# A hybrid streaming encoder layer: a small table moved behind four large slots, and three subtractions moved from VectorE to GpSimd

## The chip, the cores and the metric

One core of one Trainium2 chip runs the whole layer. The metric is the device time of one execution in microseconds; lower is better.

## The reference

One layer of a trunk with three gated branches, for 1024 prompt rows and 32 sample rows of width 1024, in float32:

```python
xn = rmsnorm(h, norm_mix)
proj = xn @ w_in
u_a, u_b, v_b, q, k, v, gates = jnp.split(proj, IN_SPLITS, axis=-1)
y_a, st_re, st_im = s5_mixer(u_a, ...)
y_b, vn_b = sgu_mixer(u_b, v_b, sgu_norm, sgu_w, sgu_b)
...
y_c = o.transpose(0, 2, 1, 3).reshape(bsz, L, SB_WIDTH).astype(h.dtype)
g = jax.nn.sigmoid(gates.astype(jnp.float32)).reshape(bsz, L, N_BRANCH, D_MODEL)
merged = (g[:, :, 0] * (y_a @ w_branch_a) + g[:, :, 1] * (y_b @ w_branch_b)
          + g[:, :, 2] * (y_c @ w_branch_c))
h = h + (merged.astype(h.dtype) @ w_out).astype(h.dtype)
gu = rmsnorm(h, norm_ffn) @ w_gate_up
h = h + ((jax.nn.silu(gate) * up) @ w_down).astype(h.dtype)
```

`o` is stick-breaking attention of 8 heads of 64 over 1024 positions: the weight of position s for query t is `exp(log_sigmoid(z_s) + sum of log_sigmoid(-z) over the positions between s and t)`, and it multiplies the values.

## The kernel before

**Split operands.** Every dense product is made of three matmuls (`mm3`, lines 143 to 146): an operand a is stored as a high part, rounded to float32r, and a low part a - high; the product is ah·bh + ah·bl + al·bh. A split costs one copy on ScalarE for the high part and one subtraction for the low part, on VectorE (DVE) or GpSimd (POOL).

**Stages.** In this order: normalise and turn x; project values, queries and keys, the S5 branch and the gated MLP branch; attention, with the remaining dense work (keys, queries, gates ahead) dealt out between its steps by `fill`; the gates and branch outputs (`gates`, per half of the rows); the output projection (`out_proj`); the up projection (`up_tile`, 22 tiles, each of seven products for two chunks of 256 and 272 columns); the down projection (`down_groups`, 11 groups of 256 hidden columns, the last two done together) and the final norm. A scheduler sets the order on each engine from priorities; TensorE's order of the up projection is written out by hand.

**Attention.** For each pair of heads hp, each quarter tp of the queries and each head h2 of the pair there is a unit: scores (lines 824 to 828), sigmoid into `om` on ScalarE (line 830), a running product backwards over `om` on VectorE (the scan of line 832), turning of `om` on TensorE (line 854) into PSUM, high parts `wth` or `wd` on ScalarE (line 862), low parts `wtl` or `wd` on VectorE (line 863), products with the values (lines 871 and 872). The sum over the weights is rewritten by parts, so what multiplies the weights is not the values but differences of neighbouring values. `differences` (lines 785 to 791) makes them once for each of the 8 heads: line 787 subtracts shifted values (128x512), line 789 does the four diagonal blocks with their last row, line 790 rounds the high part on ScalarE, line 791 makes the low part (128x768) into `vt`. The raw values `va` have one buffer, `vt` three. After the second head of each pair, 16 times in all, lines 884 to 887 add the two halves of the output (64x512), split it, and store it with two DMAs on SP's queue (line 890); `yo` has one buffer.

```python
for i in range(2):
    ahead(i)
...
for i, u in enumerate(units):
    ahead(i + 2)
```

`ahead` loads the queries of the unit two places on and, when it is the first of its head, its keys and values; the differences of that head are recorded at the next call.

**Memory of the later stages.** Behind each other in each partition lie the pool `late` (`hS`, `mt2`, `gb`, `ss2`, `htmp`) and the pool `hy` of four slots of 17408 bytes. `ss2` holds 20 numbers in each partition: the sums of squares of the rows for the norm in front of the up projection. It takes 80 bytes, rounded up to 96. In the built program the four slots `hy` begin at bytes 140512, 157920, 175328 and 192736, each 32 past a multiple of 64; the four slots of the older pool `hx` begin at 17536, 34944, 52352 and 69760, multiples of 128; the rings of split weights `wh` and `wl` begin at multiples of 128 too. In `hy` lie `y` and `m` of the gates (`m` is the stationary operand of the output projection), `xo2` to `xo5` of the up projection (moving operands; `xo0`, `xo1` and `xo6` lie in `hx`), and `act` of ten of the eleven groups of the down projection, the stationary operand there. The first group's `act` is put into `hx` (`load_act(0, wa, hx)`). The stationary `xn` of the values' projection lies in `hx`.

Of the kernel before, what the change touches and what calls it, by code (L numbers as in the profile page):

```python
# [9 lines left out]
F32 = mybir.dt.float32  # L10
# [38 lines left out]
def trunk_kernel(ctx: ExitStack, tc: tile.TileContext,  # L49
# [7 lines left out]
    v, g, s, pe, sp = nc.vector, nc.gpsimd, nc.scalar, nc.tensor, nc.sync  # L57
    PSUM, DRAM = bass.MemoryType.PSUM, bass.MemoryType.DRAM

    def pool(name, bufs=1, space=None):  # L60
        if space is DRAM:
            return tc.tile_pool(name=name, bufs=bufs, space=space)
        if space is not None:
            return tc.tile_pool(name=name, bufs=bufs, space=space, reuse_waits="tile")
        return tc.tile_pool(name=name, bufs=bufs, reuse_waits="tile")
# [138 lines left out]
    with ExitStack() as ph1:  # L204
# [6 lines left out]
        def ps_tile(tag):  # L211
            return ps1.tile([128, 512], F32, name="p_" + tag, tag=tag)
# [550 lines left out]
        def attention(at, qk_tasks):  # L763
# [20 lines left out]

            def differences(va, vt):
                vb = vt[:, :, 1, :].bitcast(F32)
                v.tensor_sub(va[:, 0:8], va[:, 0:8], vb[:, 0:8])

                v.scalar_tensor_tensor(va[:, 8:12], vb[:, 8:12], last, va[:, 8:12], op0=OP.mult, op1=OP.add)
                s.activation(vt[:, :, 0, :], va, AF.Copy)  # L790
                v.tensor_sub(vt[:, :, 1, :], va, vt[:, :, 0, :].bitcast(F32))

            heads = {}

# [43 lines left out]
            def stage_b(hp, tp, h2, ws):  # L838
                vt = heads[hp, h2][1]
                if h2 == 0:  # L840
                    avs[hp, tp] = ps_tile("av")
                av2 = avs[hp, tp]
                av = av2[:, 256 * h2:256 * h2 + 256]
                hl = {}

                def turn(p):

                    pt = ps_tile("t")
                    diag = p == tp
                    for e in range(4):  # L850
                        if diag and e == 0:
                            continue
                        sb, tt = 2 * p + 1 - e // 2, e % 2
                        pe.transpose(pt[:, 128 * e:128 * e + 128], ws[tt][:, 128 * sb:128 * sb + 128], ident)
                    lo = 128 if diag else 0
                    if diag:
                        wh, wl = diags[cnt[0] % 2]
                        cnt[0] += 1
                    else:
                        wh = at.tile([128, 512], F32R, name="wth", bufs=2)  # L860
                        wl = at.tile([128, 512], F32R, name="wtl", bufs=2)
                    s.activation(wh[:, lo:512], pt[:, lo:512], AF.Copy)
                    v.tensor_sub(wl[:, lo:512], pt[:, lo:512], wh[:, lo:512].bitcast(F32))
                    hl[p] = wh, wl

                def apply(p):
                    wh, wl = hl.pop(p)
                    for i in range(2):
                        b = 8 + p if p == tp and i == 0 else 2 * p + 1 - i
                        lhs = vt[:, b].rearrange("p l d -> p (l d)")  # L870
                        pe.matmul(av, lhs, wh[:, 256 * i:256 * i + 256], start=(p == 0 and i == 0), stop=False)
                        pe.matmul(av, lhs, wl[:, 256 * i:256 * i + 256], start=False, stop=(p == tp and i == 1))

                for p in range(tp + 1):
                    turn(p)
                    yield 0.44
                    if p:
                        apply(p - 1)
                        yield 0.44
                apply(tp)  # L880
                if h2:
                    yo = at.tile([64, 2, 512], F32R, name="yo")
                    ty = yo[:, 1].bitcast(F32)
                    s.activation(ty, av2[64:128], AF.Copy)
                    v.tensor_add(ty, av2[0:64], ty)
                    s.activation(yo[:, 0], ty, AF.Copy)
                    v.tensor_sub(yo[:, 1], ty, yo[:, 0].bitcast(F32))
                    o = 256 * (tp % 2)
                    for e in range(2):
                        sp.dma_start(y_d[4 + hp][tp // 2].rearrange("l p t -> p l t")[64 * e:64 * e + 64, :, o:o + 256],  # L890
                                     yo[:, :, 256 * e:256 * e + 256].bitcast(F32))
                yield 0.44
# [9 lines left out]
            def ahead(i):  # L902

                if i < len(units):
                    hp, tp, h2 = units[i]
                    new = (hp, h2) not in heads
                    if new:
                        finish(qk_tasks[hp])
                        heads[hp, h2] = [load_head(hp, h2)]
                    load_q(hp, tp, h2)  # L910
                    if new:
                        while raw_values:
                            differences(*raw_values.pop())
                        pair = load_values(hp, h2)
                        heads[hp, h2].append(pair[1])
                        raw_values.append(pair)
                        return
                while raw_values:
                    differences(*raw_values.pop())
# [5 lines left out]
            for i, u in enumerate(units):  # L925
                ahead(i + 2)
                nxt, done = None, True
                if i + 1 < len(units):
                    nxt = stage_a(*units[i + 1])
                    done = False  # L930
                for c in stage_b(*u, ws):
                    fill(ratio * c)
                    if not done:
                        try:
                            wn, c = next(nxt)
                            fill(ratio * c)
                        except StopIteration:
                            done = True
                if not done:
                    for wn, c in nxt:  # L940
                        fill(ratio * c)
                if nxt is not None:
                    ws = wn
                if i == 30:
                    sample_attention(at)
# [124 lines left out]
    late = ctx.enter_context(pool("late", 1))  # L1070
# [8 lines left out]

    H = [None, None]  # L1080

    ss2 = late.tile([128, 20], F32, name="ss2")
    v.memset(ss2, 0.5)

    def h_rows(b):
# [441 lines left out]
```

## Time and profile before

| | |
|---|---|
| time, median of 3 runs | 1766.96 us (1764.95 to 1767.31) |
| the profiled execution's own time | 1750.41 us |
| its span | 1748.7 us |
| TensorE matmul busy (PE) | 1642.2 us, 94% |
| VectorE busy (DVE) | 974.5 us, 56% |
| ScalarE busy (ACT) | 603.3 us, 35% |
| GpSimd busy (POOL) | 626.5 us, 36% |

The page gives the busy time of each engine and cuts the span into 40 slices of 43.7 us. A share of busy time is a mean over stages with different limits. Matmuls are pipelined: the record of one lasts longer than the distance from its start to the next one's start, so the pace is read from starts. PE is TensorE's matmul, PEld its loading of the stationary operand.

### The profile page before, as it was taken

Reading aid. Unit: us, or ns where it says so; the run is one execution under the profiler, and the core shown is the slowest. Engines: PE = TensorE matmul, PEld = TensorE weight load, DVE = VectorE, ACT = ScalarE, POOL = GpSimd, SP = SyncE. Lnnn points to the kernel's source line nnn. Section 1 sums busy time; section 2 is a strip of 40 time slices with the busy share of each in tenths; the row PEclk is TensorE's granted clock in tenths of the full one; section 3 lists DMA queues with packets and bytes.
Section 4 is the critical chain, followed back from the end, with each engine's and each line's share of the span. In section 5 each row is a group of like instructions: output and inputs, shape, how many; then the busy total and the mean of one; then the engine's idle time right before and its main releaser. Section 6 shows DMA issues by size and latency. Waiting matters only on the chain. (4 is left out here: it accounts for less than half of the span.)

```text
span 1748.7 us, 28070 instructions
## 1 busy us (share of the span) xinstructions
PE 1642.2 (94%) x10949; PEld 1489.0 (85%) x10949; DVE 974.5 (56%) x1864; ACT 603.3 (35%) x1111; POOL 626.5 (36%) x378
## 2 busy tenths in 40 slices
PE   6989998999889899999999798999999999899997
PEld 6978896778677798899999798999999998677775
DVE  7963513512899730910284756666555556566545
ACT  4322332233667532223225543333333323222114
POOL 2310211433102223434456754333333326544434
PEclk9999999999999999999999899999999999999999
DMA  7454245356656427854361223322222226322212
GB/s 225 108 134 93 84 137 129 97 169 192 172 150 160 119 80 239 261 193 133 92 214 49 81 79 109 94 77 74 74 80 85 83 85 233 109 75 79 67 37 88
DMA packets 271421, 211.57 MB, mean 121 GB/s; under 512 B 68340, under 2 KB 244504, under 8 KB 270776
## 3 DMA queue, kind: packets, MB, share of 16 engines
q1 hardware_dynamic: 242728, 194.56, 37.9%
q10 hardware_dynamic: 28560, 15.21, 2.9%
q8 instruction: 86, 1.41, 0.4%
q14 instruction: 47, 0.39, 0.1%
HBM read 153.83 MB, written 55.30 MB: 120 GB/s over the span
## 5 line engine op out<-in xcount | busy, mean ns | idle before, releaser
L118 POOL TENSOR_TENSOR wl<-raw,wh 128x1024 fp32r<-128x1024 f32 x120 | 303.3, 2535 | 735.1 <-ACT wh L117 695.0
L117 ACT ACTIVATE wh<-raw 128x1024 fp32r<-128x1024 f32 x120 | 126.3, 1058 | 331.1 <-PE p L146 146.4
L144 PE MATMUL p<-xo,wl 128*128 128x256 f32 (+1 forms) x616 | 178.0, 289 | 5.9 <-DVE fs L1353 3.2
L144 PE MATMUL p<-xo,wh 128*128 128x256 f32 (+1 forms) x616 | 177.5, 288 | 4.0 <-ACT wh L1308 2.3
L146 PE MATMUL p<-xo,wl 128*128 128x256 f32 (+1 forms) x616 | 178.0, 289 | 3.3 <-POOL wl L1309 3.3
L146 PE MATMUL p<-xo,wh 128*128 128x256 f32 (+1 forms) x616 | 178.0, 289 | 2.2 <-POOL wh L1309 2.2
L145 PE MATMUL p<-xo,wh 128*128 128x256 f32 (+1 forms) x616 | 176.6, 287 | 1.2 <-POOL xo L1247 1.2
L145 PE MATMUL p<-xo,wl 128*128 128x256 f32 (+1 forms) x616 | 176.5, 287 | 0.0
L144 PE MATMUL p_d<-xnh,wh 128*128 128x272 f32 (+1 forms) x464 | 157.8, 340 | 6.5 <-ACT wh L117 3.5
L146 PE MATMUL p_d<-xnh,wl 128*128 128x272 f32 (+1 forms) x464 | 155.4, 335 | 5.0 <-POOL wl L118 5.0
L145 PE MATMUL p_d<-xnl,wh 128*128 128x272 f32 (+1 forms) x464 | 155.2, 334 | 0.0
L144 PE MATMUL p<-wh,act 128*128 128x512 f32 x352 | 140.7, 400 | 5.9 <-DVE htmp L136 3.6
L1481 DVE TENSOR_TENSOR hd<-p,hd 128x512 f32<-128x512 f32 x160 | 107.1, 684 | 70.1 <-PE p L146 69.7
L145 PE MATMUL p<-wl,act 128*128 128x512 f32 x352 | 140.7, 400 | 2.4 <-POOL wl L118 2.4
L146 PE MATMUL p<-wh,act 128*128 128x512 f32 x352 | 140.5, 399 | 0.0
L1309 POOL TENSOR_TENSOR wh<-raw,wh 128x512 fp32r<-128x512 f32 x59 | 79.3, 1347 | 139.0 <-ACT wh L1308 137.6
L1309 POOL TENSOR_TENSOR wl<-raw,wl 128x512 fp32r<-128x512 f32 x58 | 78.6, 1358 | 135.2 <-ACT wl L1308 134.6
L144 PEld LDWEIGHTS p<-xo,wl 128*128 128x128 f32 x616 | 117.7, 191 | 7.0 <-DVE fs L1353 3.4
L144 PEld LDWEIGHTS p<-xo,wh 128*128 128x128 f32 x616 | 117.9, 191 | 4.8 <-ACT wh L1308 2.6
L146 PEld LDWEIGHTS p<-xo,wl 128*128 128x128 f32 x616 | 117.8, 191 | 3.7 <-POOL wl L1309 3.7
L146 PEld LDWEIGHTS p<-xo,wh 128*128 128x128 f32 x616 | 117.8, 191 | 2.5 <-POOL wh L1309 2.4
L145 PEld LDWEIGHTS p<-xo,wh 128*128 128x128 f32 x616 | 118.3, 192 | 1.4 <-POOL xo L1247 1.4
(463 smaller groups left out, 4415.2 us busy)
## 6 DMA issues: line engine op xcount, KB each, us to landing
raw<-in_w_in_dram SPq DMA_DIRECT2D x66, 512.0 KB, 4.0
raw<-in_w_gate_up_dram SPq DMA_DIRECT2D x46, 512.0 KB, 4.4
ra<-act_d SPq DMA_DIRECT2D x22, 528.0 KB, 4.1
raw<-in_w_down_dram SPq DMA_DIRECT2D x22, 512.0 KB, 3.8
q<-q_d SPq DMA_DIRECT2D x64, 128.0 KB, 2.9
raw<-in_w_out_dram SPq DMA_DIRECT2D x16, 512.0 KB, 6.0
act_d<-fs SPq DMA_DIRECT2D x44, 128.0 KB
act_d<-fa SPq DMA_DIRECT2D x44, 128.0 KB, 3.9
```

The lines of the kernel that those rows point to most:

```text
L117: s.activation(wh, raw, AF.Copy)
L118: g.tensor_sub(wl, raw, wh.bitcast(F32))
L144: pe.matmul(ps, ah, bh, start=start, stop=False)
L145: pe.matmul(ps, ah, bl, start=False, stop=False)
L146: pe.matmul(ps, al, bh, start=False, stop=stop)
L1309: eng.tensor_sub(lo, src, hi.bitcast(F32))
L1481: v.tensor_add(hr[:, cs], ps, hr[:, cs])
```

## The change

Three subtractions of the attention go to GpSimd (`g`) in place of VectorE (`v`): the differences of shifted values (line 787), their low parts (line 791) and the low parts of the attention outputs (line 887). Their number and shapes stay: 8, 8 and 16. The table `ss2` gets a pool of its own, opened after `hy`, so that it lies behind the four slots.

```diff
             def differences(va, vt):
                 vb = vt[:, :, 1, :].bitcast(F32)
-                v.tensor_sub(va[:, 0:8], va[:, 0:8], vb[:, 0:8])
+                g.tensor_sub(va[:, 0:8], va[:, 0:8], vb[:, 0:8])
...
-                v.tensor_sub(vt[:, :, 1, :], va, vt[:, :, 0, :].bitcast(F32))
+                g.tensor_sub(vt[:, :, 1, :], va, vt[:, :, 0, :].bitcast(F32))
...
-                    v.tensor_sub(yo[:, 1], ty, yo[:, 0].bitcast(F32))
+                    g.tensor_sub(yo[:, 1], ty, yo[:, 0].bitcast(F32))
...
-    ss2 = late.tile([128, 20], F32, name="ss2")
+    ss2 = ctx.enter_context(pool("late2", 1)).tile([128, 20], F32, name="ss2")
```

In the built program `ss2` then lies at byte 210048, in memory that the last of the four buffers of `om` held before (it was memory of `k32`), and `hy` begins 96 bytes earlier: 140416, 157824, 175232 and 192640, all multiples of 128. `hx`, the rings and the tiles of the attention stay where they were. TensorE's order changes in the attention alone, where dense matmuls fall between other steps than before.

On VectorE, at the start of the attention (`om` is the running product of line 832, `wd` and `wtl` low parts of turned weights, `va` and `vt` raw values and their differences):

```order
 L832 SCALAR_TENSOR_TENSOR om<-om 128x256
 L863 TENSOR_TENSOR wd_3835<-p_t,wd_3834 128x384
-L787 TENSOR_TENSOR va<-va,vt 128x512
 L789 SCALAR_TENSOR_TENSOR va<-vt,last,va 128x256
-L791 TENSOR_TENSOR vt<-va,vt 128x12x64
 L832 SCALAR_TENSOR_TENSOR om<-om 128x128
 L832 SCALAR_TENSOR_TENSOR om<-om 128x256
 L863 TENSOR_TENSOR wd_3837<-p_t,wd_3836 128x384
-L787 TENSOR_TENSOR va<-va,vt 128x512
 L789 SCALAR_TENSOR_TENSOR va<-vt,last,va 128x256
-L791 TENSOR_TENSOR vt<-va,vt 128x12x64
```

Line 789 stays on VectorE and stands between scans, now without the subtraction in front of it and the one behind it.

On GpSimd, from the start of the attention (`wl` is the low part of a unit of dense weights, line 118):

```order
-L118 TENSOR_TENSOR wl<-raw,wh 128x1024 x9
+L118 TENSOR_TENSOR wl<-raw,wh 128x1024
+L787 TENSOR_TENSOR va<-va,vt 128x512
+L791 TENSOR_TENSOR vt<-va,vt 128x12x64
+L787 TENSOR_TENSOR va<-va,vt 128x512
+L791 TENSOR_TENSOR vt<-va,vt 128x12x64
+L887 TENSOR_TENSOR yo<-yo 64x512 x2
+L787 TENSOR_TENSOR va<-va,vt 128x512
+L791 TENSOR_TENSOR vt<-va,vt 128x12x64
+L887 TENSOR_TENSOR yo<-yo 64x512
+L118 TENSOR_TENSOR wl<-raw,wh 128x1024
```

GpSimd had nothing but weights' low parts here; now 787, 791 and 887 stand in its one line with them.

On SP's queue, at the third and fourth quarter of the second pair of heads (`q` are queries, `va` and `vt` values, `y_d` the stored outputs):

```order
 L781 DMA va<-v_d_73 128x8x64
-L806 DMA q_4832<-q_d_64 64x2x256
 L890 DMA y_d_0_121<-yo 64x2x256 x2
-L806 DMA q_4832<-q_d_64 64x2x256
+L806 DMA q_4832<-q_d_64 64x2x256 x2
+L806 DMA q_4917<-q_d_65 64x2x256 x2
 L782 DMA va<-v_d_73 128x4x64
-L806 DMA q_4917<-q_d_65 64x2x256 x2
 L781 DMA vt<-v_d_73 128x8x64
+L890 DMA y_d_0_121<-yo 64x2x256 x2
```

The stores of the outputs have moved by a place or two against the loads of queries and values.

## Rows read from the trace of the kernel before

**Rows 1.** Page, busy tenths of VectorE in 40 slices of the span.
```profile
DVE  7963513512899730910284756666555556566545
```

**Rows 2.** Windows: start:end, length, busy us (instructions) of PE, PEld, DVE, ACT, POOL; granted clock.
```profile
444.00:582.00 138.00, 121.29 (x815) 101.25 (x813) 132.85 (x151) 91.70 (x183) 22.07 (x5) 0.99 0.62 158
582.00:655.00 73.00, 69.08 (x522) 64.79 (x523) 34.21 (x51) 29.48 (x59) 17.51 (x22) 0.98 0.30 89
```

**Rows 3.** Waits from 444 to 582 us: us in total, times, longest.
```profile
PEld p_av L872 <- DVE wtl L863: 15.8, 20, 3.0
```

**Rows 4.** Timeline of PE, down projection: start, duration (us).
```profile
1464.46 0.39 PE L144 MATMUL p<-wh,act 128*128 128x512 f32 x1
...
1475.11 0.39 PE L146 MATMUL p<-wh,act 128*128 128x512 f32 x1
...
1550.06 0.40 PE L146 MATMUL p<-wh,act 128*128 128x512 f32 x1
...
1561.07 0.39 PE L145 MATMUL p<-wl,act 128*128 128x512 f32 x1
```

**Rows 5.** Timeline of PE, output projection and values' projection.
```profile
750.29 0.28 PE L144 MATMUL p<-wh,m 128*128 128x256 f32 x1
...
783.89 0.28 PE L144 MATMUL p<-wh,m 128*128 128x256 f32 x1
...
59.28 0.28 PE L144 MATMUL p_av<-wh,xnh 128*128 128x256 f32 x1
...
62.13 0.28 PE L144 MATMUL p_d<-wh,xnh 128*128 128x256 f32 x1
```

**Rows 6.** Timeline of PE, up projection: one product from xo4, one from xo6.
```profile
1175.44 0.29 PE L144 MATMUL p<-xo,wh 128*128 128x272 f32 x1
...
1176.93 0.28 PE L144 MATMUL p<-xo,wh 128*128 128x256 f32 x1
...
1178.38 0.29 PE L144 MATMUL p<-xo,wh 128*128 128x272 f32 x1
...
1179.88 0.28 PE L144 MATMUL p<-xo,wl 128*128 128x256 f32 x1
```

**Rows 7.** Groups of VectorE, 444 to 582 us: count, busy us, mean ns.
```profile
L887 DVE TENSOR_TENSOR yo<-yo 64x512 fp32r<-64x512 f32 x12 | 8.1, 672 | 0.9 <-ACT yo L886 0.6
...
L791 DVE TENSOR_TENSOR vt<-va,vt 128x768 fp32r<-128x768 f32 x6 | 6.7, 1121 | 0.1
L787 DVE TENSOR_TENSOR va<-va,vt 128x512 f32<-128x512 f32 x6 | 5.1, 853 | 0.0
```

**Rows 8.** Groups of GpSimd by shape, whole span: count, busy us, mean ns.
```profile
L1309 POOL TENSOR_TENSOR wh<-raw,wh 128x512 fp32r<-128x512 f32 x59 | 79.3, 1347 | 139.0 <-ACT wh L1308 137.6 <-issue 1.4
...
L1390 POOL TENSOR_TENSOR act<-ra,act 128x1024 fp32r<-128x1024 f32 x22 | 53.1, 2421 | 14.4 <-ACT act L1389 14.4
L1475 POOL TENSOR_TENSOR hS<-hS,htmp 32x512 f32<-32x512 f32 x20 | 25.6, 1278 | 12.6 <-DVE htmp L136 11.5 <-DVE rs_m L170 1.1
```

**Rows 9.** Timeline of VectorE, rows beside GpSimd's five and two undisturbed ones.
```profile
476.32 2.02 DVE L791 TENSOR_TENSOR vt<-va,vt 128x768 fp32r<-128x768 f32 x1
478.27 2.58 DVE L832 TENSOR_TENSOR_SCAN om<-om 128x128 f32<-128x128 f32 x1
...
522.36 0.41 DVE L832 TENSOR_TENSOR_SCAN om<-om 128x128 f32<-128x128 f32 x1
...
552.84 2.27 DVE L832 TENSOR_TENSOR_SCAN om<-om 128x1024 f32<-128x1024 f32 x1
...
559.19 2.63 DVE L832 TENSOR_TENSOR_SCAN om<-om 128x1024 f32<-128x1024 f32 x1
...
567.77 3.28 DVE L832 TENSOR_TENSOR_SCAN om<-om 128x1024 f32<-128x1024 f32 x1
...
572.01 1.74 DVE L787 TENSOR_TENSOR va<-va,vt 128x512 f32<-128x512 f32 x1
```

**Rows 10.** Groups of GpSimd, 444 to 582 us.
```profile
L118 POOL TENSOR_TENSOR wl<-raw,wh 128x1024 fp32r<-128x1024 f32 x5 | 22.1, 4433 | 122.9 <-ACT wh L117 122.9
```

## The prediction

> **What bounds the kernel now.** I read the page's engine slices first, then the windows of the two places that the change touches, then the waits, then single rows. TensorE is busy for nearly all of the span (the table above), so a gain has to shorten TensorE's own work or take away one of its waits. VectorE's slices [rows 1] show one stretch, the 11th to the 14th slice, in which VectorE is full: that is the attention stage. The windows give its edges [rows 2]: from 444 to 582 us VectorE is busy 132.85 of 138.00 us and GpSimd 22.07, while TensorE has 121.29; from 582 to 655 VectorE is down to 34.21 of 73.00 us. So in the first stretch VectorE sets the pace, in the second it has time to spare. TensorE's longest wait in the stretch says the same [rows 3]: 15.8 us of weight loads waiting for line 863, VectorE's low parts of the turned weights. The last stages (gates, output projection, up and down projections) are TensorE's alone, and there a gain can only come from faster matmuls.
>
> **The change, part one: the 96 bytes.** The table `ss2` leaves the pool in front of the `hy` slots, and the built program moves all four slots from 32 bytes past a multiple of 64 to multiples of 128. The `hx` slots are multiples of 128 in both. No instruction is added or moved by this. The trace of before holds a natural experiment: the same matmuls run out of both kinds of slot.
>
> Down projection, stationary operand `act`. The first group's `act` lies in `hx`: from 1464.46 to 1475.11 there are 47 steps from start to start, 10.65 / 47 = 0.2266 us each. The fourth group's lies in `hy`: 1550.06 to 1561.07, 47 steps again, 11.01 / 47 = 0.2343 us [rows 4]. Ten of the eleven groups have their `act` in `hy`, with 16 products of 6 matmuls each for the prompt's rows: 960 matmuls x 0.0077 = 7.4 us less, if address is the cause. TensorE has no gaps inside these groups, so it counts in full. The 64-column matmuls of the sample rows are few (80); I leave them at nothing, at most 80 x 0.0077 = 0.6 us.
>
> Output projection, stationary operand `m`, 256 columns, in `hy`: 288 steps from 750.29 to 783.89, 33.60 / 288 = 0.1167 us. The same shape with `xn` stationary out of `hx`: 24 steps from 59.28 to 62.13, 2.85 / 24 = 0.1188 us [rows 5]. Here the slot that is off by 32 bytes is the quicker one. There are 768 such matmuls: 768 x 0.0021 = 1.6 us more.
>
> Up projection, moving operand `xo`, 272 columns: twelve matmuls out of `xo4` (`hy`) take 1176.93 - 1175.44 = 1.49 us, twelve out of `xo6` (`hx`) 1179.88 - 1178.38 = 1.50 [rows 6]. Five of the seven products of a tile use `hy` slots for this chunk: 22 x 5 x 0.01 = 1.1 us more. The 256-column products and the gates' `y` operands have no clean pair of rows; I take them at nothing, within 1.2 us either way (576 gate matmuls at the 0.0021 of rows 5).
>
> Sum of part one: -7.4 + 1.6 + 1.1 = -4.7 us. Its ends: 0 if the address is not the cause, -8 if only the down projection reacts.
>
> **Part two: VectorE gives three subtractions to GpSimd.** In the full stretch it loses 12 of line 887 (8.1 us), 6 of 791 (6.7) and 6 of 787 (5.1), 19.9 us together [rows 7]. Two of these hold a collision each, about 1.1 us, which would hit the next instruction instead (below), so 19.9 - 2.1 = 17.8 us of pace. The other moved ones (4 of line 887, 2 of each of the others) lie outside, where VectorE has time: nothing.
>
> GpSimd gets the work at its own price. Its 32x512 subtraction takes 1278 ns and its 128x512 one 1347 [rows 8]; for 64x512 I take 1.3 us, for line 787 1.35. Line 791 has 768 elements, half way between 1347 and the 2421 ns of 1024: 1.89. In the stretch: 12 x 1.3 + 6 x 1.35 + 6 x 1.89 = 35.0 us, on an engine that is busy 22.07 of 138.
>
> That is not free for VectorE. In the stretch, five low parts of weights (line 118) ran on GpSimd [rows 10], 2.4 us each when nothing is in the way (the same size in rows 8). Five VectorE rows with both inputs in SBUF grew beside them [rows 9]: line 791 at 476.32 (2.02; the other five average 0.94 by rows 7), the scan at 478.27 (2.58, against 0.41 at 522.36), the scans at 559.19 and 567.77 (2.63 and 3.28, against 2.27 at 552.84), line 787 at 572.01 (1.74, the other five 0.68). That is 1.08 + 2.17 + 0.36 + 1.01 + 1.06 = 5.7 us for 5 x 2.4 = 12.0 us of GpSimd: 47%. In between, rows that read PSUM (lines 863, 885) ran on untouched, which is why it isn't all of it. So the 35.0 us cost VectorE 35.0 x 0.47 = 16.5, and part two is -17.8 + 16.5 = -1.3 us. Its ends: -16.7 (no collisions; TensorE's busy time leaves no more, 138.00 - 121.29) and +17.2 (35.0 - 17.8, each GpSimd instruction costs all its length). I keep to the 47%, since those rows are this stretch and this pair of engines.
>
> The Trainium skill (SBUF — State Buffer, section "Who interferes with whom") states that a VectorE instruction with two SBUF inputs and a GpSimd instruction that reads SBUF lock each other out for the whole instruction; the five rows agree in kind, and by that rule alone, with a two-input instruction always next, part two would be the +17.2 of the upper end.
>
> What else the move touches. Line 789 now waits on VectorE for GpSimd's line 787, and behind it stand scans; 787 needs only its two loads, and GpSimd reaches it early, so I take nothing. Line 791 comes later by 1.89 - 0.94 = 0.95 us; TensorE waits for no `vt` in rows 3's view, and the heads are loaded two units ahead: nothing, but up to 0.95 + 0.67 us (787's share) at each of the three places where a head pair begins, 4.9 us, if that lead is used up. The output `yo` has one buffer: line 884 on ScalarE may wait for its stores if line 887 stands behind a 791. Each of the 32 stores on SP's queue now waits for GpSimd, and query loads stand behind them; these are for two units on. Nothing for both, by the same lead. The `memset` of `ss2` now waits for the last buffer of `om` instead of `k32`; behind it on VectorE are gates that TensorE reaches only after more dense work: nothing.
>
> **Sum.** -4.7 - 1.3 = -6.0 us. Against the profiled execution, 1750.41 - 6.0 = 1744.4; that execution lies 0.9% below the median of the runs, 1766.96, so the same 6.0 us there give **1761.0 us**, 0.34% less. About 0.2%, 3.5 us, is what a measurement of this kernel can tell from no change.
>
> **The rivals.** *The address is not the cause.* Part one is then 0, and the time 1766.96 - 1.3 = 1765.7. For it: the first group could be quick because its slot lies far from the weights, and the up projection's rows hardly differ. Against it: rows 5 and 6 differ by slot too, and with opposite sign, as one cause of distance would not make them. The Trainium skill (TensorE: Matmul & The Clock Gate, section "Wait — 56ns, not 53.3ns?") gives the spacing of warm matmuls as columns / 2.4 GHz plus some 2.5 ns, with no address in it; by that rule this rival holds, but the rows at 0.2266 and 0.2343 have the same columns and both lie above it. Chance 0.20.
>
> *GpSimd's instructions cost VectorE nearly all their length*, as the scan at 478.27 did (2.17 of 2.4). It happens where a scan follows a scan and no PSUM row stands between. At all of it the time is 1766.96 - 4.7 + 17.2 = 1779.5. It ends slower by over 3.5 us from a share of (17.8 + 4.7 + 3.5) / 35.0 = 74%. Against it: four of the five rows lost 15 to 45%. Chance 0.17.
>
> *The collisions hide behind PSUM rows.* The new instructions are shorter than 2.4 us, and two PSUM rows cover 1.3. At a share of 15%, the smallest of the five, part two is -17.8 + 5.2 = -12.6 and the time 1749.7. Against it: TensorE and ScalarE would have to follow at once. Chance 0.13.
>
> **How the numbers follow.** The forecast has 0.50; the uncertain 1.6, 1.1 and the bounds of the small terms spread it from about 1756 to 1766, two thirds of that below 1763.4. So faster by over 0.2%: 0.33 + 0.13 = 0.46. Within: 0.17 of the forecast and 0.17 of the first rival, 0.34. Slower: 0.17 and the 0.03 of the first rival with a bad part two, 0.20. The range of 8 in 10 runs from 1753 to 1774; it leaves out the better half of the third case and the worse part of the second. The forecast's own range is 1756 to 1766.
>
> **What would show it.** Down groups two to eleven at 0.2266 us a step; output projection at 0.1188; `xo4` products at 1.50. In the stretch that is now 444 to 582 us, VectorE rows of lines 787, 791 and 887 gone, scans longer by some 16 us in sum, the stretch about as long as before. I am wrong if the down steps stay at 0.2343, or if the stretch changes by more than 5 us.

## The result, and the profile after

The changed kernel took 1767.56 us, median of 20 runs; the kernel before, run beside it, 1755.8 us, median of 20. The ratio is 1.006 with a 95% interval of 1.0035 to 1.0085: slower by 6 to 15 us, where 6.0 us less was forecast.

One run of the changed kernel, of 2640.7 us at a granted clock of 0.557, is not in the ratio, and the other runs of both kernels fall into two clusters some 13 us apart, by the granted clock in a stretch ahead of the attention where both programs are the same (0.94 from 300 to 360 us in the profiled execution of before, 0.72 in that of after). So stages are compared below and not spans. From the first product of line 824 the two executions stand so:

| stage | before, us | after, us | difference |
|---|---|---|---|
| attention: first product of line 824 to last of line 872 | 219.0 | 235.6 | +16.6 |
| gates and branch outputs, to the first product of `m` | 93.8 | 95.5 | +1.7 |
| output projection, to the first product of `xo` | 231.8 | 231.0 | -0.8 |
| up projection, to the first product of `act` | 486.4 | 487.8 | +1.4 |
| down projection, to the end | 290.3 | 285.1 | -5.2 |

The sum is +13.7 us, and more than all of the loss is attention. Its length repeats well: six other programs of this study with the attention code of before, profiled in either cluster, had 218.0 to 220.7 us, so differences of two microseconds say nothing and those of five do. All that follows the attention took 1097.4 to 1103.5 us in the eleven programs that leave the operands' addresses alone; there only differences of more than six say something by themselves, and smaller ones need the steps behind them.

**The later stages.** The timeline of TensorE after: one down group's first and 48th matmul (its fourth, as in [rows 4]); a run of 358 output matmuls and its end ([rows 5]); one `xo4` product of 272 columns and the row behind it ([rows 6]).

```profile
1574.03 0.39 PE L144 MATMUL p<-wh,act 128*128 128x512 f32 x1
...
1584.71 0.39 PE L146 MATMUL p<-wh,act 128*128 128x512 f32 x1
...
777.94 0.28 PE L144 MATMUL p<-wh,m 128*128 128x256 f32 x1
...
820.50 0.29 PE L144 MATMUL p<-xnh,wh 128*128 128x272 f32 x1
...
1265.92 0.29 PE L144 MATMUL p<-xo,wh 128*128 128x272 f32 x1
...
1267.43 0.28 PE L144 MATMUL p<-xo,wl 128*128 128x256 f32 x1
```

The down step is 10.68 / 47 = 0.2272 us (0.2343 before), the output projection's 42.56 / 358 = 0.1189 (0.1167), the product 1.51 (1.49 to 1.50). These are the forecast's three effects, each with its sign. The stages show only the first of them: the output projection took 228.5 to 232.1 us in the eleven programs with `m` at its old place, so the 1.7 us of its step don't stand out.

**The attention.** Windows of before and then of after, cut at the same work: at the first product, at the first scans of head pairs 1, 2 and 3, at the first scan of the fourth unit of pair 3, and at the end. Columns as in [rows 2].

```profile
427.39:478.30 50.91, 46.96 (x283) 37.64 (x283) 40.05 (x48) 29.22 (x58) 5.13 (x3) 1.00 0.67 174
478.30:522.40 44.10, 38.02 (x254) 32.40 (x254) 41.54 (x51) 25.99 (x54) 2.26 (x1) 0.96 0.58 149
522.40:563.80 41.40, 37.48 (x253) 30.98 (x252) 40.31 (x52) 29.44 (x58) 6.08 (x2) 1.00 0.64 167
563.80:594.30 30.50, 26.26 (x195) 23.77 (x195) 26.17 (x28) 18.75 (x36) 11.81 (x3) 1.00 0.56 137
594.30:646.40 52.10, 49.33 (x371) 45.54 (x370) 23.06 (x38) 20.29 (x43) 12.72 (x20) 0.97 0.30 89
```

```profile
441.88:494.90 53.02, 46.05 (x252) 36.20 (x253) 35.20 (x38) 26.43 (x54) 16.29 (x10) 0.94 0.58 145
494.90:537.60 42.70, 37.10 (x256) 30.86 (x255) 37.13 (x44) 27.23 (x56) 17.85 (x9) 1.00 0.55 146
537.60:590.30 52.70, 41.07 (x262) 34.60 (x261) 45.74 (x45) 30.75 (x60) 21.16 (x11) 0.92 0.55 135
590.30:626.00 35.70, 30.76 (x212) 28.45 (x213) 26.79 (x23) 18.53 (x37) 13.54 (x8) 0.92 0.59 147
626.00:677.50 51.50, 48.61 (x373) 44.64 (x372) 22.17 (x35) 20.48 (x43) 16.93 (x23) 1.00 0.32 91
```

The third and fourth stretch carry the loss: 11.3 and 5.2 us. In the third VectorE is busy for 45.74 us with seven instructions fewer (40.31 with 52 before): what stayed on it grew. TensorE's own busy time rose too, by 3.6 and 4.5 us, in part with more matmuls (262 for 253, 212 for 195) and in part at a granted clock of 0.92 where it had 1.00. What grew on VectorE over the whole attention, and what GpSimd's new instructions took, by groups (before first, then after):

```profile
L832 DVE TENSOR_TENSOR_SCAN om<-om 128x128 f32<-128x128 f32 (+3 forms) x64 | 88.8, 1399 | 16.6 <-ACT om L830 16.4
L789 DVE SCALAR_TENSOR_TENSOR va<-vt,last,va 128x256 f32<-128x256 f32 x8 | 3.8, 472 | 0.0
```

```profile
L832 DVE TENSOR_TENSOR_SCAN om<-om 128x128 f32<-128x128 f32 (+3 forms) x64 | 105.1, 1655 | 28.3 <-ACT om L830 28.0
L789 DVE SCALAR_TENSOR_TENSOR va<-vt,last,va 128x256 f32<-128x256 f32 x8 | 7.3, 917 | 0.8 <-DMA vt<-v_d 0.5 <-POOL va L787 0.2
L887 POOL TENSOR_TENSOR yo<-yo 64x512 fp32r<-64x512 f32 x15 | 28.5, 1901 | 68.9 <-ACT yo L886 68.9
L791 POOL TENSOR_TENSOR vt<-va,vt 128x768 fp32r<-128x768 f32 x8 | 14.8, 1852 | 16.3 <-ACT vt L790 15.0 <-DMA q<-q_d 1.3
L787 POOL TENSOR_TENSOR va<-va,vt 128x512 f32<-128x512 f32 x8 | 14.1, 1764 | 22.7 <-DMA vt<-v_d 13.0 <-DMA va<-v_d 7.2 <-issue 2.4
```

The scans took 16.3 us more, almost the 16.5 of the forecast, and line 789 another 3.5. GpSimd was held as well: line 887 took 1.90 us and line 787 1.76, against the 1.3 and 1.35 I had taken (line 791 took 1.85, for 1.89). VectorE, relieved, now waits 28.0 us for ScalarE's sigmoids instead of 16.4. TensorE's waits in the attention, before and then after:

```profile
PE p_av L872 <- DVE wtl L863: 13.6, 17, 2.8
PE p_t L854 <- DVE om L832: 5.7, 13, 0.9
```

```profile
PE p_av L872 <- DVE wtl L863: 12.9, 15, 2.7
PE p_t L854 <- DVE om L832: 12.4, 13, 2.8
PE p_av L871 <- ACT wth L862: 3.2, 2, 2.9
...
PE p_av L871 <- POOL vt L791: 1.6, 2, 1.0
```

The wait for line 863, which I had read as the sign of VectorE's pace [rows 3], hardly shrank; the wait for the scans more than doubled, and waits for ScalarE and GpSimd are new. How one of them comes about stands in the timeline of after, engine by engine (start, duration, idle time before and its releaser):

```profile
584.33 1.30 POOL L887 TENSOR_TENSOR yo<-yo 64x512 fp32r<-64x512 f32 x1 [6.58 <-ACT yo L886]
585.60 2.36 POOL L118 TENSOR_TENSOR wl<-raw,wh 128x1024 fp32r<-128x1024 f32 x1
...
584.58 3.65 DVE L789 SCALAR_TENSOR_TENSOR va<-vt,last,va 128x256 f32<-128x256 f32 x1
...
588.33 0.84 ACT L790 ACTIVATE vt<-va 128x768 fp32r<-128x768 f32 x1 [3.12 <-DVE va L789]
589.08 0.58 ACT L862 ACTIVATE wth<-p_t 128x512 fp32r<-128x512 f32 x1
...
586.54 0.29 PE L146 MATMUL p_d<-xnh,wl 128*128 128x272 f32 x1
589.71 0.58 PE L871 MATMUL p_av<-wth,vt 128*128 128x256 f32 x1 [2.87 <-ACT wth L862]
590.09 0.79 PE L824 MATMUL p_z<-kst,q 128*128 128x512 f32 x1
```

GpSimd runs line 887 and, without a gap, a low part of weights. VectorE's line 789, 0.47 us long otherwise, starts beside them and ends at 588.23, behind both. ScalarE stands at line 790, which needs it, and the high part `wth` behind it on ScalarE comes late; TensorE stands for 2.87 us, and the 256-column matmul after that takes 0.58 us where such rows took 0.28 before the wait. The window from there (columns as in [rows 2]) shows the granted clock at 0.50, the lower of its two levels (1.2 of 2.4 GHz):

```profile
589.71:596.00 6.29, 6.29 (x26) 5.68 (x27) 6.29 (x5) 2.89 (x6) 1.36 (x1) 0.50 0.66 133
```

One collision has passed through three queues.

### The profile page after: what moved, and what is told of

The parts are those of the page before. It is cut to its first block, busy times and chain, and to the rows that moved or that the text cites. A ratio compares the mean times of both kernels' runs of the same rounds, so it can differ in the third digit from the quotient of the medians.

```text
span 1776.9 us, 28128 instructions
## 1 busy us (share of the span) xinstructions
PE 1658.2 (93%) x10949; PEld 1506.5 (85%) x10949; DVE 965.7 (54%) x1832; ACT 602.9 (34%) x1111; POOL 674.9 (38%) x410
## 5 line engine op out<-in xcount | busy, mean ns | idle before, releaser
L118 POOL TENSOR_TENSOR wl<-raw,wh 128x1024 fp32r<-128x1024 f32 x120 | 294.8, 2463 | 602.5 <-ACT wh L117 558.7
L144 PE MATMUL p<-wh,act 128*128 128x512 f32 x352 | 138.3, 393 | 6.5 <-DVE htmp L136 4.2
L146 PE MATMUL p<-wh,act 128*128 128x512 f32 x352 | 138.3, 393 | 0.0
L144 PEld LDWEIGHTS p<-xo,wh 128*128 128x128 f32 x616 | 118.9, 193 | 4.7 <-ACT wh L1308 2.6
L146 PEld LDWEIGHTS p<-xo,wh 128*128 128x128 f32 x616 | 118.8, 193 | 2.5 <-POOL wh L1309 2.4
L832 DVE TENSOR_TENSOR_SCAN om<-om 128x128 f32<-128x128 f32 (+3 forms) x64 | 105.1, 1655 | 28.3 <-ACT om L830 28.0
```

The costliest lines, as they stand in the source:

```text
L118: g.tensor_sub(wl, raw, wh.bitcast(F32))
L144: pe.matmul(ps, ah, bh, start=start, stop=False)
L146: pe.matmul(ps, al, bh, start=False, stop=stop)
L832: v.tensor_tensor_scan(rev, rev, rev, 1.0, op0=OP.mult, op1=OP.bypass)
```

## Experiments

All are edits of the kernel before, and attention is read from the first product of line 824 to the last of line 872.

**1. The address alone** (`e1_address`): the last part of the diff and nothing else. 

> Only the table of sums of squares goes behind the four slots; the three subtractions stay on VectorE. If the start address of the matmul operands is what changed the later stages: down steps at 0.2271 us, output projection at 0.1189, up products of 272 columns at 1.516, together 4 to 5 us less time (faster by 0.25%). If those stages owe it to the different attention ahead of them: steps as in the kernel before (0.2342, 0.1167, 1.495) and no change of the time. The attention takes as long as in the kernel before in both cases, within 2 us.

1757.93 us, median of 12 runs, against 1760.95; ratio 0.9977 (0.9943 to 1.0011). Down steps 0.2269, output 0.1189, `xo` products of 272 columns 1.517; the last stage 282.7 us instead of 290.3, output and up projection 1.0 and 0.7 us longer. By these three stages 5.9 us are gained; the interval of the times holds that and also holds nothing. That the gain is real rests on the steps.

**2. GpSimd alone** (`e2_three_gp`): the three lines of the diff with `g.` and nothing else. 

> Only the three subtractions go to GpSimd; the table stays in front of the slots. If the two parts add up: 14 to 17 us more (the changed kernel's 10 and the 4 to 5 that the address gives back), all of it between the first and the last product of the attention, and down steps at 0.2342. If the new attention also costs the later stages something (a wait that the new pool adds), less than 12 us.

1778.78 us; ratio 1.0094 (1.0057 to 1.0131), 16.6 us more. Attention 235.4 us (+16.4), down steps 0.2342, and TensorE's order is that of the changed kernel, matmul for matmul. As far as times so wide can tell, the two parts add (-4.0 and +16.6 alone, some +10.5 together).

**3. Relief without work** (`e3_left_out`):

```diff
-                v.tensor_sub(va[:, 0:8], va[:, 0:8], vb[:, 0:8])
-                v.tensor_sub(vt[:, :, 1, :], va, vt[:, :, 0, :].bitcast(F32))
-                    v.tensor_sub(yo[:, 1], ty, yo[:, 0].bitcast(F32))
```

> The three subtractions are not made by any engine: the differences of values, their low parts and the low parts of the attention outputs stay what the loads and the sums left there. This shows what VectorE's relief alone is worth. Theory A (VectorE's full stretch sets the pace, so the relief is worth its 17.8 us, and GpSimd's instructions cost more than 47% of their length): 14 to 18 us less. Theory B (the relief is worth little, because the chain from scores to scan to turned weights to values sets the pace and the three subtractions only filled VectorE's time beside it): 0 to 5 us less. Theory C (VectorE's relief is worth 17.8 us, but ScalarE and TensorE wait for GpSimd's late results): 14 to 18 us less.

Ratio 0.9954 (0.9916 to 0.9992). The window of its attention:

```profile
429.54:643.61 214.07, 195.18 (x1348) 166.43 (x1349) 150.79 (x179) 122.69 (x247) 30.77 (x27) 1.00 0.57 146
```

VectorE is busy 20 us less than before, the attention is 5.0 us shorter: 2.9 us less TensorE busy time, at a clock of 1.00 instead of 0.98, and 2.1 us fewer waits. Nobody waits for the three lines' results here either, so 5.0 is the most that relief can give. Most of TensorE's 21 us of idle time are not VectorE's to give back. Theories A and C fall on this point. Where VectorE's 20 us went, its waits show; first the second of them in the kernel before (the first was 16.4 us there), then both in this run:

```profile
DVE wtl L863 <- ACT wth L862: 7.9, 7, 2.3
```

```profile
DVE om L832 <- ACT om L830: 27.6, 9, 13.1
DVE wtl L863 <- ACT wth L862: 15.6, 15, 2.3
```

It stood 18.9 us longer for ScalarE's sigmoids and high parts.

**4. Work without relief** (`e4_doubled`): VectorE keeps its lines, and ahead of each GpSimd makes a copy of it.

```diff
+                g.tensor_sub(scr.rearrange("p a (b c) -> p a b c", c=64), ...)
                 v.tensor_sub(va[:, 0:8], va[:, 0:8], vb[:, 0:8])
...
+                g.tensor_sub(scr.rearrange("p a (b c) -> p a b c", c=64), vh, vh)
                 v.tensor_sub(vt[:, :, 1, :], va, vt[:, :, 0, :].bitcast(F32))
...
+                    g.tensor_sub(scr[0:64], yh, yh)
                     v.tensor_sub(yo[:, 1], ty, yo[:, 0].bitcast(F32))
```

> The three subtractions stay on VectorE, and GpSimd makes a subtraction of its own beside each (16 of 64x512, 16 of 128x512, some 41 us at about 1.28 each), from operands that are there at the same points, into columns that nobody reads until the samples' keys overwrite them. This shows what GpSimd's work alone costs. Theory A (GpSimd's instructions cost VectorE nearly their length): 28 to 38 us more. Theory B (they cost what the scans grew by, some 16 us, and the relief gives little back): 13 to 20 us more. Theory C (the cost is the lateness of GpSimd's results, and here nobody waits for one): 0 to 5 us more.

Ratio 1.0075 (1.0036 to 1.0115); attention 233.6 us, 14.5 more. That is Theory B's range, but the run is not quite free of waits for GpSimd: line 791 (line 794 of this kernel) overwrites what the first copy (`KS`, line 787 here) reads, and VectorE waited for that.

```profile
DVE vt L794 <- POOL KS L787: 3.9, 3, 2.0
```

So the 14.5 may hold up to some 4 us that are not GpSimd's work beside VectorE. TensorE's order is that of the kernel before but for three matmuls, so order is not the cause.

**5. Work and relief, and nobody waits** (`e10_copies_only`): the copies of experiment 4, the lines of experiment 3 left out. 

> No engine makes the three subtractions that the kernel needs, and GpSimd makes the same 32 subtractions of its own as in the doubled kernel, whose results nobody reads. So VectorE has its relief and GpSimd's instructions run, but ScalarE, TensorE and the stores wait for none of GpSimd's results. Attention, first to last product: 219.0 us before, 214.1 with the three left out, 233.6 with them doubled, 235.4 with the three on GpSimd. Theory B (relief and GpSimd's cost add, and the rest of the 235.4 is waiting for GpSimd's late results): 219.0 - 5.0 + 14.5 = 228.6 us. Theory D (nobody waits for the results in a way that counts; the relief is worth nothing once GpSimd's instructions run between the scans): 233 to 236 us. Theory A (the relief is worth its 17.8 us as soon as VectorE is slowed down by GpSimd): 233.6 - 17.8 = 216 us.

```profile
428.56:652.64 224.08, 198.16 (x1348) 169.52 (x1349) 159.67 (x179) 122.86 (x247) 81.61 (x58) 0.98 0.54 139
```

Attention 224.1 us; ratio 1.0001 (0.9963 to 1.0039). None of the three had it: 4.5 us under B's 228.6, about what experiment 4's own wait may be worth. TensorE's order is exactly that of experiment 3, so the 10.0 us between the two are GpSimd's work. And the run splits the loss: to 235.4 us, with the same relief and nearly the same work on GpSimd, 11.3 us are missing, and what the change has and this run has not is that stores, VectorE, ScalarE and TensorE depend on GpSimd's results. Not all of that need be plain waiting: the copy for line 791 is a third shorter, the scans took 107.9 us in experiment 2 and 100.9 here, and the two runs' orders on TensorE differ.

**6. Line by line.** Line 887 alone (`e5_887_gp`), lines 787 and 791 (`e6_values_gp`), 791 alone (`e7_791_gp`), 787 alone (`e6_787_gp`), and copies in place of line 887 (`e15_887_copy`) or of 787 and 791 (`e16_values_copy`).

> Only the low parts of the attention outputs (line 887) go to GpSimd: 16 instructions, 20.8 of the 45 us that GpSimd gets in the change. If the loss of 16.4 us goes by GpSimd's time: attention 219.0 + 7.6 = 226.6 us. If it is the waiting for late differences of values: 219 to 222. If it is the single buffer of the output (ScalarE's line 884 waits for stores that wait for GpSimd): 230 or more.

> Only the differences of values and their low parts (lines 787 and 791) go to GpSimd: 16 instructions, 24 to 26 of the 45 us. If the loss goes by GpSimd's time: attention 219.0 + 8.8 = 227.8 us. If it is the waiting for late differences: 230 or more, and rows of TensorE that wait for line 791 at the six places where a head pair begins. If it is the output's single buffer: 219 to 222.

> Of the three subtractions only the low parts of the values (line 791) go to GpSimd, 8 instructions. Attention 219.0 us before, 234.2 with lines 787 and 791 on GpSimd. If the loss comes from TensorE waiting for late low parts of values and the clock lost in these waits: 228 us or more, with rows of TensorE that wait for line 791. If it comes from ScalarE's and VectorE's queues standing still behind the chain of line 787, 789 and 790: 219 to 224, and no such rows.

> Of the three subtractions only line 787 goes to GpSimd, 8 instructions of about 1.3 us. Line 791 alone cost 4.3 us of attention, 787 and 791 together 15.1. If their costs add: 219.0 + 10.8 = 230 us. If the chain of both (787 on GpSimd, 789 on VectorE, 790 on ScalarE, 791 on GpSimd) is what costs: 219 to 224 us.

> Line 887 is left out on VectorE (the low parts of the attention outputs are not made), and GpSimd makes a subtraction of the same size at the same point whose result nobody reads. Against the run with line 887 on GpSimd (attention 231.0 us) only the waiting for its result goes: the stores and, through the single output buffer, ScalarE's line 884. Theory C (the late result is what costs): 219 to 223 us. Theory B (GpSimd's work beside VectorE's scans is what costs): 228 to 231 us.

> Lines 787 and 791 are left out on VectorE (the values stay undifferenced but for line 789, and their low parts are what the load left), and GpSimd makes 16 subtractions of 128x512 at the same points whose results nobody reads. Against the run with both lines on GpSimd (attention 234.2 us) the waiting for their results goes. Theory C (late results): 219 to 224 us. Theory B (GpSimd's work itself): 230 to 234 us.

| on GpSimd | attention, us | TensorE busy, us | the same as copies nobody reads, us |
|---|---|---|---|
| 787 | 219.5 | 198.9 | |
| 791 | 223.4 | 197.4 | |
| 787 and 791 | 234.2 | 203.5 | 222.1 |
| 887 | 231.0 | 200.2 | 222.5 |
| all three | 235.4 | 201.6 | 224.1 |

The ratios of `e5_887_gp` and `e6_values_gp` are 1.0052 (1.0018 to 1.0087) and 1.0039 (1.0004 to 1.0075). Theory C holds for both halves: with copies the cost is 3.5 and 3.1 us, with the real lines 11.9 and 15.1. Line 887 alone also met its forecast for the single output buffer (230 or more). Neither line of the values is dear alone (0.5 and 4.4 us); both together are, where the chain is 787 on GpSimd, 789 on VectorE, 790 on ScalarE, 791 on GpSimd. With line 791 alone TensorE waited for it at four places, 3.6 us in all, which its second theory had excluded; with both lines it was four places again and not six, but 6.9 us, and TensorE was busy 4.7 us longer than with the copies. These two make nearly all of the 12.1 us between 234.2 and 222.1. From the run with both lines, the sum of these waits and the longest of them, on GpSimd and on TensorE; then GpSimd and ScalarE from the run with line 887:

```profile
PE p_av L871 <- POOL vt L791: 6.9, 4, 3.5
...
542.37 4.58 POOL L791 TENSOR_TENSOR vt<-va,vt 128x768 fp32r<-128x768 f32 x1 [7.24 <-PE p_z L828]
...
547.00 0.58 PE L871 MATMUL p_av<-wd,vt 128*128 128x256 f32 x1 [3.49 <-POOL vt L791]
```

```profile
501.50 4.40 POOL L887 TENSOR_TENSOR yo<-yo 64x512 fp32r<-64x512 f32 x1 [9.04 <-ACT yo L886]
...
509.08 0.59 ACT L884 ACTIVATE yo<-p_av 64x512 f32<-64x512 f32 x1 [3.48 <-DMA y_d<-yo]
```

In the first, line 791 took 4.58 us on GpSimd beside VectorE's scans, where it takes 1.80 undisturbed; TensorE waits for these low parts of a new head's values and then runs at a granted clock of 0.50 (547 to 552 us). In the second, GpSimd's subtraction took 4.40 us instead of 1.28, while VectorE's scan of 512, line 791 and scan of 384 ran at their usual 1.21, 0.93 and 0.94 us; the stores of the one output buffer left late, and ScalarE stood 3.48 us at the next output with the high parts of the weights queued behind it.

**7. What the address does.** First the activations moved by 32 bytes inside their slots (`e8_act_aligned`), then each group at its own start (`e11_scan`), then the same with the weights moved too (`e13_scan_w64`).

```diff
-        act = p.tile([128, 2, 2 * T], F32R, name="act", tag="hx" if p is hx else "hy")
+        o = 0 if p is hx else (0, 40, 8, 56, 24, 0, 48, 16, 32, 40, 40)[gr]
+        act = p.tile([128, 4 * T + 64], F32R, name="act", tag="hx" if p is hx else "hy")
+        act = act[:, o:o + 4 * T].rearrange("p (e c) -> p e c", e=2)
```

(In `e8_act_aligned` the offset is 8 numbers, and `e13_scan_w64` has a tile of 16 numbers in front of the pool of weights.)

> The attention and the table stay as in the kernel before; only the activations of the down projection start 32 bytes further into their slot where the slot is one of the four off-aligned ones, so they start at multiples of 128 as in the changed kernel, while the operands of the output and up projections keep their old places. If only the start address counts: down steps at 0.2271, output projection at 0.1162 to 0.1180 and up products as in the kernel before; the last stage 283 to 285 us instead of 290.3, the whole time 5 to 7 us less than before, 2 to 3 us better than the table behind the slots gives. If the slot's place matters and not the 32 bytes: 0.2342 and no change.

> Attention and table as in the kernel before. Each of the down projection's groups two to nine has its activations start at another multiple of 32 within 256 bytes: in this order at 128, 0, 192, 64, 224, 160, 32 and 96 past a multiple of 256, groups ten and eleven (done together) at 128. The weights that move through start at 128 past a multiple of 256 in all. What the runs have shown: 128 gives 0.2270 us a step, 0 gives 0.2321, 224 gives 0.2341. If quick means only a start at 128 past a multiple of 256: 0.2270 in groups two, ten and eleven alone. If every place between has its own step: eight levels. If what counts is the slot in which the activations lie and not their start: 0.2341 throughout.

> As the scan before, with a pad of 64 bytes in front of the ring of weights and all that lies behind it: the moving weights now start at 192 past a multiple of 256, and the activations of groups two to eleven at 192, 64, 0, 128, 32, 224, 96, 160, 192, 192. If the step hangs on the distance between the two operands' starts: the same steps group by group as in the scan without the pad, 0.2270 in groups two, ten and eleven. If it hangs on the activations' own address: 0.2270 in group five (128), and 0.2321 in group four (0).

In `e8_act_aligned` the starts are multiples of 128, as in the changed kernel, and the step is 0.2324, not 0.2270 (ratio 0.998, 0.9942 to 1.0019): multiples of 128 were not the cause. The scans gave, per group, the mean from start to start; distance is the start of `act` less that of the moving weights, modulo 256 bytes:

| distance, bytes | 0 | 32 | 64 | 96 | 128 | 160 | 192 | 224 |
|---|---|---|---|---|---|---|---|---|
| us a step, `e11_scan` | 0.2270 | 0.2332 | 0.2332 | 0.2343 | 0.2325 | 0.2333 | 0.2289 | 0.2333 |
| us a step, `e13_scan_w64` | 0.2269 | 0.2332 | 0.2332 | 0.2343 | 0.2325 | 0.2333 | 0.2289 | 0.2333 |

With the weights 64 bytes on, every group keeps the step of its distance and not that of its own address. Even the first group, in the old slot, went from 0.2269 to 0.2290, because its distance went from 0 to 192.

**8. A better version** (`e12_act160`, `e14_pad64_act0`): attention and table as before, all `act` at distance 0; in the second also the pad in front of the weights. 

> The kernel before with one edit: the activations of the down projection start 160 bytes into the four slots, at 128 past a multiple of 256, as in the changed kernel; everything else keeps its place. If the start within 256 bytes is what counts: down steps at 0.2270 in all groups, the last stage 282 to 285 us long instead of 290.3, output and up projections as before, so 6 to 8 us less than before and 15 to 18 less than the changed kernel. If not: 0.2321 as with 32 bytes, 2 to 3 us less than before.

> The kernel before with two edits: a pad of 64 bytes in front of the ring of weights, and all activations of the down projection at distance 0 (modulo 256) from the weights that move against them (64 bytes into the old slots, 160 into the four younger ones). If the distance of the two operands is what counts: all down steps at 0.2270 (6 us less than before), the up projection's products of 256 columns out of the two oldest slots at 0.1155 instead of 0.1193 as in the scan with the pad (4 us less), attention within 2 us of before; together 9 to 12 us less than the kernel before and some 20 less than the changed kernel. If the up projection's gain came from something else in the scan: 5 to 7 us less than before.

`e12_act160`: all down steps 0.2270, last stage 284.3 us, others as before; 1756.01 us, ratio 0.9973 (0.9934 to 1.0013). `e14_pad64_act0`: 1757.49 us, ratio 0.998 (0.994 to 1.002). A product of 256 columns out of `xo0` in its timeline, and the row behind:

```profile
1232.17 0.28 PE L144 MATMUL p<-xo,wh 128*128 128x256 f32 x1
...
1233.56 0.29 PE L144 MATMUL p<-xo,wh 128*128 128x272 f32 x1
```

Twelve matmuls take 1.39 us, where the same product took 1.43 before. By stages, from the first product of line 824 to the end: 1311.0 us against 1321.3 of before and 1335.0 of the changed kernel, so 10 and 24 us less. The median times do not show the 10 apart from nothing. All behind the attention took 1091.9 us here, against the 1097.4 to 1103.5 of the eleven programs with the old addresses: 5 to 12 us less, which the steps bear out.

## Why the prediction was wrong

**Part one came in the direction that was forecast; its size is in part luck.** Forecast -4.7; alone it gave -4.0 by the times, with an interval from -10 to +2, and -5.9 by its three stages. By the steps it is less: down 960 x (0.2342 - 0.2269) = 7.0 us less for 7.4, output 768 x 0.0022 = 1.7 more for 1.6, and up some 3.1 more for 1.1. The up term failed since every 272-column product took 1.517 us with the new addresses, those out of `xo6` as well, whose slot stayed, where I had taken its 1.50 of before as the level to come: per tile 0.124 us for the seven, times 22 = 2.7, and 0.4 for 256 columns. That sums to -2.2 us. The rule I read from [rows 4 to 6], that the slots differ by where they begin, had the right rows and the wrong reason: what counts is the distance from the other operand. Experiment 7 has the case: starts moved by 32 bytes alone are multiples of 128 too, I would have forecast 0.2266 for them, and the step was 0.2324. The rival of the address that doesn't matter falls. The Trainium skill ("TensorE: Matmul & The Clock Gate", section "Wait — 56ns, not 53.3ns?") gives the spacing of warm matmuls by their columns alone; here 512 columns had eight starts and five levels of spacing, 0.2270 to 0.2343, and the measurement decides.

**Part two was wrong by 17.7 us**, in all three of its terms:

| term | forecast, us | measured, us | by |
|---|---|---|---|
| VectorE's relief | -17.8 | -5.0 (at most) | experiment 3 |
| GpSimd's work beside it | +16.5 | +10.0 | experiment 5 less 3 (224.1 - 214.1) |
| dependence on GpSimd's results | 0 | +11.3 | experiment 2 less 5 (235.4 - 224.1) |
| sum | -1.3 | +16.4 | |

- The step "VectorE sets the pace" failed. 132.85 of 138.00 us busy [rows 2] and a wait of 15.8 us [rows 3] showed VectorE full. They did not show that a shorter VectorE lets the others run: scores, sigmoid, scan, turning, high part, low part and values follow one another over three engines, and VectorE without its three lines waited 18.9 us longer for ScalarE instead (experiment 3).
- The step on collisions came out near for the scans (+16.3 for +16.5), in part by luck: the forecast priced 35.0 us of GpSimd in one stretch, and over the whole attention the three lines took 57.4 us there, beside which the scans and line 789 grew by 19.8, a share of 34% and not 47%. And VectorE's growth is not the attention's growth. The rivals with 74% and 15% are beside the point. The second rival's time, 1779.5, lies near the 1777.6 that the measured ratio makes of 1766.96, but its share did not happen. I had also written of the scan at 478.27 that a scan stood ahead of it; in [rows 9] it is line 791.
- The Trainium skill ("SBUF — State Buffer", section "Who interferes with whom") says that a VectorE instruction with two SBUF inputs contends with a GpSimd instruction that reads SBUF, by an exclusive lock, and that issue order decides who blocks. Here the holding is seen on both sides: line 789 at 584.58 ended behind both GpSimd instructions, and line 887 at 501.50 behind three of VectorE's. The issue order does not explain it all: line 887's record starts 0.40 us ahead of the scan's, and yet the scan ran at its usual 1.21 us and line 887 was held.
- The step "nothing for both, by the same lead" failed most. I had named every one of these waits (line 789 behind 787, line 791 late, `yo` with one buffer, the stores) and covered them by the loads two units ahead. The loads are ahead; the chain of differences behind them is not: TensorE waited 6.9 us for line 791 in the run with both lines, and ScalarE 3.48 us for one store in the run with line 887. And I priced GpSimd's instructions as if alone (1.3 us), while they were held too; [rows 10] showed it already, with 4433 ns for a low part of weights that takes 2.4 us undisturbed. The loads of queries were rightly put at nothing (1.2 us of waiting before, 2.0 after).
- A term I did not have: of the 11.3 to 11.5 us, 3.4 (experiment 2) to 5.4 (the changed kernel, 203.56 - 198.16) are TensorE busy for longer on the same matmuls. The clock granted over the attention was 0.97 and 0.96 there, 0.98 in experiment 5; in the two places shown it fell to 0.50 at a long wait.

What stays open: why the halves don't add (8.5 and 12.1 us apart, 11.3 together), and how the 11.3 divide into waits and longer collisions. The scheduler also orders TensorE's instructions a little otherwise in most of these programs. By the traces 199 of its matmuls stand elsewhere in the changed kernel than before; with as many or nearly as many (219, 202, 166) the programs in which nobody reads GpSimd's results took from 5.0 us less (experiment 3) to 5.1 more (experiment 5), so order alone is not the loss. A program with the old order and GpSimd's three lines was not tried.

## What to carry to other kernels

An engine that is 96% busy is worth relieving only as far as the next engine of its chain can follow, so leave the work out first and measure what is to be had. Here, moving small steps to an engine that collides with the full one cost twice, at the collision and again at each queue behind the late result; ask of every moved line who waits for it, and not only when its inputs are ready. Where matmuls have the same shape and different steps, compare both operands' starts.

## What the runs showed that was not expected

- TensorE's step hung on the distance of its two SBUF operands modulo 256 bytes: 0.2270 us at 0 and 0.2289 at 192 against 0.2325 to 0.2343 elsewhere, for 512 columns. Other shapes have other best places: the up projection's twelve matmuls of 256 columns out of `xo0` took 1.43 us with that slot at distance 0 and 1.39 at 192, and the output projection's step with `m` 96 bytes off was 0.1167 against 0.1189 at 0.
- In the changed kernel the products out of `xo0` and `xo6`, whose slots did not move, took 1.437 and 1.517 us instead of 1.432 and 1.508. The address alone (`e1_address`) does the same, so it comes with the neighbours' new addresses and not with the attention; how is not explained.
- GpSimd's 64x512 subtraction took from 1.28 to 4.51 us beside VectorE (`e5_887_gp`): the engine that is thought of as idle is held too.
